# Attention with bias: k of seven pairs transposed by DMA, two more slots on VectorE, and a new order of work from slot 66 on

## The chip, the core and the metric

The kernel runs on one core of one Trainium2 chip. A core has five engines that run side by side: TensorE (PE in the profile, its weight loads PEld), VectorE (DVE), ScalarE (ACT), GpSimd (POOL) and SyncE (SP). Here SP only issues DMAs, and POOL issues those that convert from f32 to bf16 on the way. The metric is the device time of one execution in microseconds; the time given is the median of several runs.

## What is computed

Attention with an additive bias for 4 x 8 heads of 1024 rows and 64 columns, all in f32 at the interface:

```python
batch, n_heads, seq_len, head_dim = 4, 8, 1024, 64
scores = scale * np.matmul(q, k.transpose(0, 1, 3, 2))     # scale = 1/8
scores = scores + bias                                     # bias: [1, 1, 1024, 1024]
scores_max = np.max(scores, axis=-1, keepdims=True)
attn = np.exp(scores - scores_max) / (np.sum(np.exp(scores - scores_max), axis=-1, keepdims=True) + 1e-8)
return np.matmul(attn, v)
```

## The kernel before

Two heads form a pair; there are 16 pairs, in two groups of nine and seven (GROUPS). The queries of a head are cut into eight chunks of 128. One chunk of one head is a **slot**: 256 slots in all, numbered in the order in which the program lists them. The scores of a slot, 1024 keys by 128 queries, fill two PSUM banks. There are three such places (x = 0, 1, 2; tile pl, six banks). The slots of group 1, pairs 9 to 15, begin at 144: each pair has six there before the middle part of the group, so that pair 9 begins at slot 144, pair 10 at 150, and pair 15 at 180.

The whole program is one list of tokens, the string ORDER; each engine gets its instructions in the order of the list. The function do (line 607) turns a token into instructions. A number in a token is a slot, if nothing else is said:

- F and G fill the two banks of a slot with scores (fill, line 383; matmuls of line 376). A bank is not cleared between the slots that follow one another on a place: what the next slot needs is added to what is there, with operands made for that (keys of two neighbouring heads side by side with a negated query). For this, a pair has four arrays: ko and qo (k and q transposed), and ke and qe, which hold halves of ko and negated qo from neighbouring pairs. The slots that start afresh get the bias by line 373.
- X is one exponential on ACT over both banks (exp, line 399), written to E in bf16. P and Q split a round of three slots into two exponentials of three banks each.
- f, r, s, h, c, l are the six steps by which DVE computes an exponential instead of ACT (d_steps, line 409): f reads the scores from PSUM into dy, r takes the low half into de, s squares into ds, h shifts de in place, c multiplies ds by de, and l makes the bf16 result in de. Each step works on 128 x 1024 elements. In the kernel before, 29 slots are done in this way.
- A multiplies the exponentials of a slot with v (av, line 462) into a bank po that holds up to seven slots (SIZES); a column of ones in v gives the sums. "a" or "b" on the token opens the next bank, in one of two places in PSUM. R takes the reciprocals of a finished bank and M multiplies with them and issues the stores of the output, on SP (line 664). M's tile ob has four buffers.
- T and C make the transposed arrays: T transposes eight 128 x 128 blocks of the landed k or q on PE into PSUM (px, line 277), in one of the two places that the banks po also use; C copies px to ko on DVE, or to qo with a change of sign by halves. For pairs from 9 on (EARLY), C of k also issues the two copies of ko into ke as DMAs on SP (line 603). N negates q for pairs from 9 on and issues the copies to qe. D and S are DVE steps of the early pairs.
- L and U ask for the next load of the list LOADS; L ties the load to DVE's last instruction. The loads of q and k land in four buffers each (LANDS); a load of k of pair p is asked for only when pair p - 4 is marked as freed, which C does. The arrays ko, ke, qo and qe come from rings of nine buffers (RING).

What a T and a C do for one k of pairs 9 to 15 are thus eight transposes on PE, one copy of 128 x 1024 from PSUM on DVE, and the DMAs of ke on SP. In the order before, Tk9a and Ck9 stand between X98 and X102, and Tk15a and Ck15 around X161. On SP the DMAs are issued in the order of the list, and a DMA that waits holds up those behind it.

Of the kernel before, what the change touches and what calls it, by code (L numbers as in the profile page):

```python
# [8 lines left out]
F32 = mybir.dt.float32  # L9
# [11 lines left out]
A10a Sk4 X14 F16 Dk3p0 A9 G16 Dq3p0 Tk4b X15 Dq3p1 A6 Ck4 F17 G17 X16 A8 Sq4 F18 G18 Dk4p0 X17 Tq4b V2 F19 Cq4 G19  # L21
X18 A7 A12 Sk5 A11 F20 X19 R1 G20 Dq4p1 Tk5b M1 F21 X20 G21 Ck5 F22 A15a Sq5 X21 F23 Dq4p0 G22 G23 Tq5b V3 X22 A13
Cq5 A16 F24 X23 G24 Dk5p0 F25 G25 Dq5p0 A17 X24 F26 G26 Sk6 A14 f26 X25 F27 G27 Tk6b X27 F28 Dq5p1 G28 Sq6 A19 A18
X28 Ck6 F29 G29 F30 R2 Dk6p0 G30 X29 F31 M2 Tq6b V4 G31 X30 F32 Cq6 G32 A20a f32 X31 A21 F33 G33 Tk7b X33 Dq6p1 F34
G34 Dq6p0 A23 Ck7 X34 F35 G35 A28 r26 F36 X35 G36 Dk7p0 F37 G37 s26 Tq7b X36 A27 Cq7 A22 A29 X37 F38 V5 G38 F39 R3
Dq7p0 G39 X38 A25b h26 F40 M3 G40 A34 X39 c26 A24 F41 A30 Dq7p1 X40 A31 l26 G41 Tk8a X41 F42 F43 Ck8 G42 G43 X42 A26
f43 F44 G44 Tq8a X44 F45 Cq8 G45 F46 X45 G46 Dk8p0 F47 A35 Dq8p0 A33a V6 X46 G47 F48 R4 G48 M4 A41 X47 F49 Sr0 G49
f48 A40 A36 X49 F50 G50 Tr0b r43 X50 A38 F51 Cr0 G51 F52 X51 A39 Dr0p3 Dq6p2 F53 G53 r48 A37 X53 G52 F54 R5 r32 G54
X52 Sr1 F56 s43 G56 X54 Dr0p1 F55 s32 Tr1b X56 M5 G55 F57 h43 G57 X55 Cr1 F59 G59 A42a Dr1p0 A56 X57 Dr1p1 F58 h32
G58 f59 A46 X58 A44 F60 G60 A45 c32 X60 F61 G61 s48 A47 F62 X61 A54b R6 L U r59 G62 A49 F63 M6 L X62 F64 G64 l32 A50  # L30
X64 A55 G63 A53a h48 A62 X63 F65 R7 c43 G65 F67 G67 M7 X65 A61 c48 L U U A51 A52 F66 s59 X67 G66 F68 G68 A60 X66 f68
L F70 G70 A58 A63b X70 F69 l43 G69 F71 A57 X69 G71 F73 l48 A67 X71 F72 G72 A66 r68 G73 X72 F74 R8 h59 G74 X73 F75 f74
L G75 A65 X75 A48 F76 G76 M8 A64 X76 F77 R9 G77 s68 A73a F78 X77 G78 c59 L F79 G79 A69 l59 L U X79 A70 F80 G80 A76
X78 f80 F82 G82 A72 A75 X82 F81 M9 G81 F83 r74 G83 X81 F85 G85 f83 A43 A71b X85 F84 G84 A81 r83 X84 F86 G86 A78 Dq8p1
L U F88 X86 s74 G88 F87 G87 s83 A82 X87 A79 h74 L F89 G89 h68 L U A77 X88 A59 F90 R11 R10 c74 G90 X89 F91 M10 G91 X90
l74 F92 X91 G92 M11 A32a F93 r80 X92 G93 A87 A91 s80 F94 X93 G94 A85 h83 F95 c68 G95 X94 A92 A74 c83 A84 F96 X95 h80
G96 A89b R12 F97 M12 G97 X96 F98 c80 A90 G98 X97 A86 l68 A88 F99 G99 X98 Tq9a A94 Cq9 F100 X99 G100 A93 l80 A68 F101
X100 G101 F102 Tk9a R13 X101 M13 G102 F103 Nq9 L G103 A96b X102 Ck9 L F104 G104 A101 f104 A97 X103 F105 G105 Tk10a
X105 l83 F106 G106 F107 G107 X106 F108 f107 G108 A80 A100 X108 F109 G109 Ck10 A99 X109 F110 G110 r107 A95 F111 X110
R14 G111 M14 A98a F112 A106 r104 X111 G112 Tq10b A103 X112 Cq10 F113 G113 A109 F114 Nq10 X113 G114 s107 Tq11b F115  # L40
X114 Cq11 G115 F116 G116 h107 L A108 X115 F117 f116 L U G117 Tk12b X117 F118 G118 Ck12 A105 A102 X118 F120 R15 G120
s104 Tk11b X120 F121 M15 G121 F119 Ck11 L G119 X121 F123 G123 f119 A83a A112 X123 F124 G124 Tq12b c107 X124 F122 Cq12
G122 F126 A110 X122 l107 L U G126 A114 F127 X126 G127 A113 r119 F125 A111 X127 G125 s119 Tk13b F129 h104 X125 G129
Ck13 A115 F130 G130 R16 X129 Nq11 L A118b F128 Nq12 A124 c104 G128 X130 A117 A123 h119 L F132 r116 G132 X128 A121
A120 l104 X132 F131 G131 F133 M16 L G133 X131 F135 G135 A130 f135 L A126a X133 F134 G134 A122 X134 A127 R17 L s116
F138 G138 F136 M17 X138 G136 F137 G137 f136 Tk14b X137 F141 G141 A129 Ck14 X141 F139 G139 c119 F140 G140 Tq14b X139
h116 r135 A104 F144 X140 Cq14 L F142 G142 A125 r136 G144 X142 A128 A137b R18 L U U F143 s136 X144 G143 F145 c116 L U
G145 A107 X145 A133 s135 F147 A132 M18 G147 X143 A131 F148 l116 A138 G148 X147 F146 A134 G146 R19 Tq13a X148 M19 F150
G150 h135 A141b X146 h136 F151 G151 Cq13 L U U A139 A116 X150 c136 F149 G149 A140 l119 X151 F153 Tq15a X149 F154 Cq15
# [5 lines left out]
F178 l152 A171 X174 F173 G178 G173 R23 A168 X178 f173 F177 G177 A172 X177 F181 M23 G181 F176 G176 X181 F180 f176 G180
A152 A175 X180 F184 G184 r173 A174 X184 F179 G179 r176 F183 A181a r164 X179 A178 G183 F187 s173 X183 G187 R24 s176
F182 G182 X187 h173 A170 F186 s164 G186 X182 c173 F190 A179 M24 X186 F185 l173 G185 A180 A155 X185 G190 F189 h164
G189 A177 X190 h176 F188 c176 G188 X189 c164 A136b A135 R25 F193 l164 X188 G193 F192 A184 G192 X193 F191 l176 G191
A187 A185 X191 F196 G196 A183 f196 X192 F194 G194 A186 X194 F195 M25 G195 F199 R26 G199 X195 F197 f199 G197 A182a
A193 X197 F198 G198 F202 f198 G202 F200 X202 G200 r196 A173 X200 F201 G201 r199 F205 G205 X201 M26 A164 F203 A190  # L60
s199 A189 X205 F204 r198 G204 A192 s196 G203 X204 F208 G208 f203 A194b A188 X208 F207 G207 A197 R27 h196 X207 F206
G206 M27 F211 A201 h199 X206 A191 s198 G211 A202 F210 r203 X211 A200 G210 A205a c196 A204 X210 F213 l196 G213 F209
A176 X213 F212 G212 c199 A196 X212 A195 G209 l199 F215 X209 G215 F214 R28 R29 s203 X215 G214 h198 F216 X214 M28 G216
M29 F218 X216 A211b h203 F217 c198 G218 A210 X218 G217 l198 A207 F219 G219 X217 F221 G221 f219 A212 A208 X221 F220
G220 c203 F222 X220 G222 F224 r219 G224 A206 X222 f224 F223 G223 A213 A220a X223 F225 R30 r224 G225 A215 X225 F227
l203 F226 G226 A214 P226 F228 s224 A222 G228 G227 h224 A216 Q226 A221 M30 A209 F229 c224 G229 A218b R31 F230 X229
l224 G230 F231 G231 A228 X230 F232 f231 G232 A199 A217 X232 F233 G233 s219 F234 A223 X233 M31 G234 F235 r231 G235
X234 F236 G236 f235 A198 A203 X236 F237 G237 A225a r235 X237 F238 F239 h219 G238 A224 R32 s235 P238 G239 A227 F240
h235 G240 A233 c219 A226 Q238 F241 M32 G241 F242 A234 c235 A232 P241 A230b l235 F243 G243 G242 A239 A238 Q241 R33
A240 l219 F244 G244 A229 F245 M33 X244 G245 F246 s231 G246 A242 X245 f246 F247 G247 A243 A237a X247 F248 h231 G248  # L70
F249 r246 A236 X248 G249 R34 F250 M34 A235 X249 F251 s246 G250 A241 A244 P250 h246 F252 G251 c231 G252 A245 c246 A219
Q250 A247b l231 F253 G253 A249 A248 F254 X253 R35 G254 M35 F255 A250 G255 l246 X254 A231 A252 A251 X255 A254a R36
A246 M36 A253 A255 R37 M37
# [19 lines left out]
def kernel(  # L93
# [404 lines left out]
    with tc.manual_schedule():  # L498
# [108 lines left out]
        def do(token):  # L607
# [21 lines left out]
            elif kind == "C":  # L629
                pr, which, c0, n = pieces[name]  # L630
                copy_out(pr, which, c0, n, rests[name])
                if which:
                    for x in parts(pr, 1):
                        if pr >= EARLY or x == 1 and pr >= 2:
                            copy(pr, x, "ke", arrs[pr]["ko"])
                    freed.add(("k", pr))
                elif pr < NEGATED:
                    freed.add(("q", pr))
                more()
            elif kind == "D":  # L640
                piece, x = name.split("p")
                pr, which, c0, n = pieces[piece]
                double(pr, which, c0, n, int(x), vec)
            elif kind == "N":
                pr = int(name[1:])
                to = negate(pr)
# [6 lines left out]
            elif kind == "V":  # L653
                pr = int(name)
# [50 lines left out]
```

## Time and profile before

| What | us |
|---|---|
| median of 3 runs | 224.58 (224.04 to 224.98) |
| span of the profiled execution, first to last instruction | 222.3 |
| median of the runs less that span (launch and end, outside the span) | 2.3 |
| ACT busy | 211.5 |
| PE busy (ends of matmuls are modelled) | 214.3 |
| DVE busy | 204.6 |
| POOL busy | 71.5 |

The profile is a record of one execution. Busy time of an engine is the time in which at least one of its instructions runs, so instructions that overlap are not counted twice: the sum of a group's busy time can be less than its count by its mean. The views used are: the page (busy times, the chain of waits, groups of instructions by line and shape), the chain in order of time (start, duration, what), the timeline (start, duration, engine, line, operation, out<-in), the waits (who waited for whom: total us, times, longest), the DMA issues (count, KB each, median us from issue to landing), and windows (for a stretch, the busy time of PE, PEld, DVE, ACT and POOL with their counts, then the granted TensorE clock, the DMA share and GB/s). In a row of a group, what stands between the bars is its busy time in us and the mean ns of one; behind the second bar stands the idle time of the engine just before them, and what ended it. All DVE operations carry line 86, since one helper records them, and are told apart by their tiles.

### The profile page before, as it was taken

How to read it: one execution, taken by the hardware profiler on the slowest of the kernel's cores; microseconds unless marked ns; L12 is line 12 of the kernel's file. 1: busy time of each engine (PE TensorE's matmuls, PEld its weight loads, DVE VectorE, ACT ScalarE, POOL GpSimd, SP SyncE). 2: the span in 40 equal slices, each digit the busy share in tenths (PEclk: the TensorE clock that was granted, in tenths of full speed). 3: DMA queues.
4: the chain of work that ended last, by engine and by line, in shares of the span. 5: the costliest groups of instructions: out<-in, count | busy, mean ns of one | idle time of the engine just before them, and what ended most of it. 6: DMA issues, size and time to landing. Idle time of an engine off the chain costs nothing.

```text
span 222.3 us, 9048 instructions
## 1 busy us (share of the span) xinstructions
PE 214.3 (96%) x3965; PEld 197.3 (89%) x3965; DVE 204.6 (92%) x354; ACT 211.5 (95%) x229; POOL 71.5 (32%) x90
## 2 busy tenths in 40 slices
PE   7799999999999999999999999999999999999993
PEld 2689999989999999999998998898988999989992
DVE  2689989999999999999998999989998999999993
ACT  2799999999999999999999999999999999999992
POOL 8825346637346563030634445341000000000000
PEclk9999999999999999999999999999999999999998
DMA  5999999999999999669999999999111122011213
GB/s 170 229 205 218 224 237 170 159 169 185 138 150 128 127 114 156 79 87 208 126 191 199 192 101 144 182 188 99 44 43 32 38 62 66 8 44 47 82 43 109
DMA packets 86343, 28.87 MB, mean 130 GB/s; under 512 B 66400, under 2 KB 83040, under 8 KB 86304
## 3 DMA queue, kind: packets, MB, share of 16 engines
q0 software_dynamic: 62880, 14.06, 69.9%
q1 hardware_dynamic: 22720, 13.44, 22.3%
q10 hardware_dynamic: 704, 0.79, 1.2%
q8 instruction: 31, 0.51, 1.0%
q14 instruction: 8, 0.07, 0.1%
HBM read 29.36 MB, written 8.39 MB: 170 GB/s over the span
## 4 chain that ended last, share of the span: by engine, by line
ACT 79%; PE 11%; DVE 5%; DMA 2%; issue 0%; SPq 0%; DVEq 0%
ACT E L399 79%; PE pl L376 6%; PE po L462 2%; DMA dy<-in_k_dram 2%; DVE de L86 1%; PE pl L373 1%; DVE qe L86 1%; PE px L277 1%; DVE ds L86 1%; DVE dy L86 1%; DVE ko L86 0%; DVE ob L86 0%; PE px L283 0%; DVE qo L86 0%; DVE ke L86 0%
## 5 line engine op out<-in xcount | busy, mean ns | idle before, releaser
L399 ACT ACTIVATE E<-pl 128x1024 bf16<-128x1024 f32 (+2 forms) x225 | 208.6, 1109 | 1.9 <-PE pl L376 1.8
L462 PE MATMUL po<-vall,E 128*128 128x65 bf16 x1816 | 86.6, 194 | 0.1
L462 PEld LDWEIGHTS <-E 128*128 128x128 bf16 x1816 | 77.0, 98 | 2.5 <-ACT E L399 0.2
L376 PE MATMUL pl<-qo,ko 128*128 128x128 bf16 (+1 forms) x752 | 77.7, 239 | 1.0 <-ACT E L399 0.3
L376 PE MATMUL pl<-qe,ke 128*128 128x128 bf16 (+1 forms) x648 | 67.2, 239 | 0.5 <-DVE qe L86 0.2
L376 PEld LDWEIGHTS <-ko 128*128 128x128 bf16 x856 | 57.3, 98 | 7.0 <-ACT E L399 3.0
L376 PEld LDWEIGHTS <-ke 128*128 128x128 bf16 x648 | 43.5, 98 | 4.6 <-ACT E L399 1.9
L86 DVE TENSOR_SCALAR dy<-pl 128x1024 int32<-128x1024 f32 x29 | 35.4, 1220 | 4.0 <-PE pl L376 3.8
L86 DVE SCALAR_TENSOR_TENSOR de<-dy,ds 128x1024 uint16<-128x1024 int32 x29 | 35.0, 1217 | 0.2
L214 POOL DMA_DIRECT2D k<-in_k_dram x18 | 16.2, 901 | 25.2 <-DVE q L86 6.4
L251 POOL DMA_DIRECT2D vall<-in_v_dram x18 | 17.8, 993 | 19.4 <-DMA vall<-in_v_dram 5.2
L214 POOL DMA_DIRECT2D q<-in_q_dram x18 | 16.0, 891 | 22.3 <-DMA out_dram<-ob 8.5
L86 DVE TENSOR_TENSOR ob<-po,rs 128x448 f32<-128x448 f32 (+3 forms) x38 | 22.7, 601 | 0.4
L86 DVE TENSOR_SCALAR de<-dy 128x1024 f16<-128x1024 uint16 x29 | 20.1, 706 | 0.1
L86 DVE TENSOR_TENSOR ds<-de 128x1024 f16<-128x1024 f16 x29 | 19.5, 675 | 0.1
L86 DVE TENSOR_TENSOR ds<-ds,de 128x1024 f16<-128x1024 f16 x29 | 19.5, 680 | 0.0
L373 PE MATMUL pl<-ident,braw 128*128 128x128 bf16 x136 | 14.0, 227 | 0.0
L86 DVE TENSOR_SCALAR qo<-px,sgn 128x1024 bf16<-128x1024 bf16 (+2 forms) x18 | 12.3, 686 | 1.5 <-PE px L277 1.4
L86 DVE TENSOR_SCALAR de<-de 128x1024 f16<-128x1024 f16 x29 | 13.1, 459 | 0.2
L462 PE MATMUL po<-vall,de 128*128 128x65 bf16 x232 | 12.4, 194 | 0.5 <-DVE de L86 0.5
L373 PEld LDWEIGHTS <-braw 128*128 128x128 bf16 x136 | 11.8, 148 | 0.4
L86 DVE COPY ko<-px 128x1024 bf16<-128x1024 bf16 (+1 forms) x16 | 10.7, 668 | 1.4 <-PE px L283 1.1
(54 smaller groups left out, 125.9 us busy)
## 6 DMA issues: line engine op xcount, KB each, us to landing
ke<-ko SPq DMA_DIRECT2D x20, 128.0 KB, 4.3
k<-in_k_dram POOLq DMA_DIRECT2D x18, 128.0 KB, 5.7
q<-in_q_dram POOLq DMA_DIRECT2D x18, 128.0 KB, 4.4
out_dram<-ob SPq DMA_DIRECT2D x24, 96.0 KB, 2.9
vall<-in_v_dram POOLq DMA_DIRECT2D x18, 128.0 KB, 5.7
out_dram<-ob SPq DMA_DIRECT2D x32, 64.0 KB, 2.8
braw<-in_bias_dram POOLq DMA_DIRECT2D x7, 256.0 KB, 6.4
de<-in_v_dram POOLq DMA_DIRECT2D x7, 256.0 KB, 7.3
```

The costliest lines, as they stand in the source:

```text
L86: i = getattr(self.engine, name)(*args, **kwargs)
L214: return nc.gpsimd.dma_start(out=t[:, :, y, :], in_=(qf, kf)[x][pr][:, y].rearrange("p (c d) -> p c d", d=D))
L251: return nc.gpsimd.dma_start(out=vall[:, (2 * pr + t) % VR, :, :D], in_=vf[pr][:, t])
L277: m = nc.tensor.transpose(px[:, c, :], raws[pr, which, c0][:, c].rearrange("p t d -> p (t d)"), ident[:])
L373: m = nc.tensor.matmul(to, braw[:, c1, :].rearrange("p (kp kc) -> p kc kp", kc=NCH)[:, kc, :], ident8[:], start=i == 0 and order[0] == "b" ...
L376: m = nc.tensor.matmul(pl[:, 2 * x + b, i * P:(i + n) * P], kk[:, kc, :], qq[:, c:c + n, :].rearrange("p c q -> p (c q)"), start=i == 0 an ...
L399: read(nc.scalar.activation(E[:, e0:e0 + n].rearrange("p b x -> p (b x)"), pl[:, b0:b0 + n].rearrange("p b x -> p (b x)"), ACTF.Exp, scale ...
L462: nc.tensor.matmul(bank[b][:, banks[b].index(s), :], weights(s, kc), vall[:, slots[s][2] % VR, kc, :], start=first and kc == 0, stop=kc == ...
```

## The change

For pairs 9 to 15, T and C of k are gone from the list. A new token K issues one transposing DMA on SP, from the landed k straight into ko, and marks k as freed; a new token J issues the copies of ko into ke, as C did before.

```diff
+            elif kind == "K":
+                pr = int(name)
+                nc.sync.dma_start_transpose(out=arrays(pr)["ko"][:], in_=raws[pr, 1, 0].rearrange("p c t d -> p (c t d)"))
+                freed.add(("k", pr))
+                more()
+            elif kind == "J":
+                pr = int(name)
+                for x in parts(pr, 1):
+                    copy(pr, x, "ke", arrs[pr]["ko"])
```

In negate, the tile is taken from lands where it is there:

```diff
-        t = raws[pr, 0, 0].rearrange("p t c d -> p (t c d)").rearrange("p (c x) -> p c x", x=P)
+        t = (lands if (pr, 0, 0) in lands else raws)[pr, 0, 0]
+        t = t.rearrange("p t c d -> p (t c d)").rearrange("p (c x) -> p c x", x=P)
```

SIZES has 38 banks as before; three of them change by one or two slots. ORDER is the same up to A60 behind G68 and new from there on. The slots from 66 on that DVE computes are now 71, 77, 83, 92, 98, 104, 113, 119, 125, 134, 140, 146, 155, 161, 167, 176, 182, 188, 197, 203, 209, 219, 225, 231, 240 and 246, 26 in place of 24 (with 26, 32, 43, 48 and 59 before them, 31 in place of 29). There is no P and no Q any more: those rounds are single X. Some lines of the old list and of the new one:

```diff
-G96 A89b R12 F97 M12 G97 X96 F98 c80 A90 G98 X97 A86 l68 A88 F99 G99 X98 Tq9a A94 Cq9 F100 X99 G100 A93 l80 A68 F101
-X100 G101 F102 Tk9a R13 X101 M13 G102 F103 Nq9 L G103 A96b X102 Ck9 L F104 G104 A101 f104 A97 X103 F105 G105 Tk10a
...
-G162 X163 s155 A148 F161 R21 A153b M21 X162 F166 G166 l135 A156 A150 X166 G161 Tk15a h155 L F165 X161 Ck15 G165 F169
...
+G99 X97 F99 f98 A93 X99 A88b F100 G100 G101 A87 R12 F101 G102 F102 A86 c83 X100 G103 A99 K12 F103 X101 G104 F104 A43
+Dq8p1 X102 L L F105 G105 l92 X103 K11 r98 f104 A101 F106 U G106 M12 X105 G107 R13 s104 A96a F107 X106 A103 G108 s98 K9
+M13 X107 F108 h98 X108 A95 G109 l83 A77 A94 F109 Tq9b Cq9 F110 c98 s104 G110 X109 A100 A97 F111 G111 F112 X110 G112
+A107b R14 Nq9 X111 F113 A102 G113 J9 F114 G114 K10 M14 f113 L Tq10a X112 Cq10 F115 G115 r113 A111 J12 X114 F116 G116
+A110 G117 F117 X115 X116 F118 G118 Nq10 A105 A112 X117 L L F119 A92 J10 X118 s113 G119 G120 F120 X120 h104 h113 A106a
...
+X136 X137 A131 F138 F139 A136 c125 X138 l113 A124 G139 G140 F140 L c119 F141 Cq12 r134 G141 X139 f140 J11 U U A130b U
+A113 G142 F142 A139 X141 X142 F143 l119 G143 R18 F144 A128 A135 G144 l125 G145 F145 K13 X143 M18 A132 G146 X144 F146
+X145 A119 Nq12 f146 G147 F147 A133a A141 J14 F148 R19 r140 s134 G148 G149 X147 r146 X148 F149 A142 G150 X149 A145 s140
+M19 G151 F150 A138 A137 F151 A83 G152 R20 X150 h140 G153 F152 Tq13b h134 X151 M20 F154 G154 J13 X152 X154 Cq13 A148a
...
+l140 Nq13 G159 X160 A144 Cq14 c134 Nq14 F161 G161 A151 s146 G163 F163 K15 X159 f161 X163 Tq15b F162 Cq15 G162 X162
+r155 F164 G164 l134 Nq15 F166 A154b A149 G166 X164 F165 G165 A152 F167 R21 G167 A153 A160 X165 J15 f167 s155 M21 G168
+F168 A158 G170 F170 X166 G169 A165 F169 X168 h146 R22 X170 A162a A157 c146 F171 X169 G171 A156 G173 F173 h155 A164
```

K14, not among these lines, stands between G138 and X136. The q of pairs 9 to 15 is still transposed by T and C.

More of the change, by code (lines that the diff above doesn't have):

```diff
@@ L20 @@
 Sk3 F11 G11 Dq2p0 Tk3b Dq2p1 X10 A3 Sq3 F12 G12 X11 Ck3 A0 A4 A1 F13 X12 R0 G13 V1 Tq3b M0 F14 X13 G14 Cq3 F15 G15
[L21 to L24, printed above, removed]
@@ L30 @@
[L30 to L34, printed above, removed]
@@ L40 @@
[L40 to L49, printed above, removed]
@@ L55 @@
[L55 to L64, printed above, removed]
@@ L65 @@
[L65 to L73, printed above, removed]
+A10a Sk4 X14 F16 Dk3p0 A9 G16 Dq3p0 Tk4b X15 Dq3p1 A6 Ck4 F17 G17 X16 A8 Sq4 F18 G18 Dk4p0 X17 Tq4b V2 F19 Cq4 G19 X18
+A7 A12 Sk5 A11 F20 X19 R1 G20 Dq4p1 Tk5b M1 F21 X20 G21 Ck5 F22 A15a Sq5 X21 F23 Dq4p0 G22 G23 Tq5b V3 X22 A13 Cq5 A16
@@ new lines @@
+F50 G50 Tr0b r43 X50 A38 F51 Cr0 G51 F52 X51 A39 Dr0p3 Dq6p2 F53 G53 r48 A37 X53 G52 F54 R5 r32 G54 X52 Sr1 F56 s43
+G56 X54 Dr0p1 F55 s32 Tr1b X56 M5 G55 F57 h43 G57 X55 Cr1 F59 G59 A42a Dr1p0 A56 X57 Dr1p1 F58 h32 G58 f59 A46 X58 A44
+F60 G60 A45 c32 X60 F61 G61 s48 A47 F62 X61 A54b R6 L U r59 G62 A49 F63 M6 L X62 F64 G64 l32 A50 X64 A55 G63 A53a h48
+A62 X63 F65 R7 c43 G65 F67 G67 M7 X65 A61 c48 L U U A51 A52 F66 s59 X67 G66 F68 G68 A60 A58 A64b G70 U X66 G69 F69 X68
+X69 F70 U A63 X70 G71 F71 A65 A68 U G72 F72 U A57 G73 h59 X72 F73 c59 l48 f71 X73 L G74 F74 F75 G75 X74 A70 F76 R8 X75
@@ new lines @@
+M8 A48 G76 X76 F77 G77 L A69a l43 F78 G78 L A32 r71 R9 s71 A74 G79 f77 L X78 F79 F80 r77 G80 F81 G81 X79 A67 M9 X80
+A72 h71 A66 A78 G82 X81 F82 G83 l59 s77 F83 A76b F84 X82 G84 A79 A73 f83 F85 G85 R10 X84 G86 X85 F86 c71 G87 A75 h77
+M10 X86 r83 l71 A80 A85 F87 X87 A84 F88 G88 A81a X88 G89 F89 G90 U X89 F90 G91 c77 R11 F91 s83 L X90 G92 L L F92 X91
+G93 F93 h83 X93 A82 l77 f92 r92 s92 L G94 F94 F95 G95 F96 M11 h92 G96 A89 A91 X94 A71 G97 F97 X95 F98 A90 G98 X96 c92
+G99 X97 F99 f98 A93 X99 A88b F100 G100 G101 A87 R12 F101 G102 F102 A86 c83 X100 G103 A99 K12 F103 X101 G104 F104 A43
@@ new lines @@
+Dq8p1 X102 L L F105 G105 l92 X103 K11 r98 f104 A101 F106 U G106 M12 X105 G107 R13 r104 A96a F107 X106 A103 G108 s98 K9
+M13 X107 F108 h98 X108 A95 G109 l83 A77 A94 F109 Tq9b Cq9 F110 c98 s104 G110 X109 A100 A97 F111 G111 F112 X110 G112
+A107b R14 Nq9 X111 F113 A102 G113 J9 F114 G114 K10 M14 f113 L Tq10a X112 Cq10 F115 G115 r113 A111 J12 X114 F116 G116
+A110 G117 F117 X115 X116 F118 G118 Nq10 A105 A112 X117 L L F119 A92 J10 X118 s113 G119 G120 F120 X120 h104 h113 A106a
+c104 f119 A116 F121 R15 G121 A115 F122 X121 r119 l98 G122 F123 A109 G123 A120 X122 A108 G124 F124 X123 X124 s119 M15
@@ new lines @@
+F168 A158 G170 F170 X166 G169 A165 F169 X168 h146 R22 X170 A162a A157 c146 F171 X169 G171 A156 G173 F173 h155 A164
+G172 X171 A159 r167 M22 l146 F172 F174 X173 A170 G174 A163 X172 G176 F176 A134b G175 F175 A173 X174 r161 F177 G177
+f176 F179 A169 R23 X175 X177 M23 c155 s161 G178 F178 X178 G179 A166 l155 s167 A171 A146 G180 X179 F180 X180 r176 A172
+G181 A168a F181 G182 F182 X181 A174 G183 F183 A140 F184 G184 f182 F185 R24 h161 G185 X183 F186 G186 h167 X184 X185
+X186 c161 F187 G187 F188 G188 G189 F189 A175 s176 l161 M24 X187 f188 X189 G190 h176 F190 X190 A184 G191 F191 A181 c167
@@ new lines @@
+X235 R32 G236 F236 A232a G237 l225 A203 X236 F238 A233 G238 X237 G239 l231 A235 A227 X238 A228 F239 X239 F240 M32 G240
+G241 F241 f240 A237 A234b G242 F242 c219 R33 X241 A231 r240 G243 F243 M33 G244 A229 A238 F244 X242 G245 F245 X243 F246
+l219 X244 G246 A236 X245 f246 G247 F247 A209 A225 F248 G248 R34 X247 r246 s240 G249 F249 X248 A244a X249 A241 M34 F250
+h240 G250 G251 F251 A248 A219 G252 A249 X250 F252 s246 A247 X251 A245 F253 c240 G253 G254 X252 A243b A242 F254 A239
+A252 h246 l240 F255 X253 G255 R35 X254 c246 A250 M35 A251 A240 l246 X255 R36 A253a A254 A246 M36 A255 R37 M37
```

33 lines of the change are left out of this document (20 added, 13 removed).

## The prediction

> **What bounds the kernel now.** I read the page's shares first, then the chain of waits in order of time, then the sums of the stretch that the change rewrites.
>
> ```profile
> span 222.3 us, 9048 instructions
> ...
> PE 214.3 (96%) x3965; PEld 197.3 (89%) x3965; DVE 204.6 (92%) x354; ACT 211.5 (95%) x229; POOL 71.5 (32%) x90
> ...
> ACT 79%; PE 11%; DVE 5%; DMA 2%; issue 0%; SPq 0%; DVEq 0%
> ...
> 47.26 114.78 ACT E L399 x125
> ...
> 172.43 44.18 ACT E L399 x45
> ...
> 66.00:218.00 152.00, 151.00 (x2795) 140.00 (x2792) 146.51 (x231) 151.68 (x162) 35.26 (x39) 1.00 0.82 105
> ```
>
> The shares alone don't choose: three engines lie between 92% and 96%. The chain does. For 114.78 and again for 44.18 us it runs from one ACT exponential to the next and leaves ACT for nothing. The last row sums the stretch that the new order covers (slot 66 starts near 66 us, the last exponentials end near 218): PE, PEld, DVE, ACT and POOL in that sequence. ACT is busy 151.68 of 152.00 us and is the bound. DVE is busy 146.51 and idle 5.5. PE's 151.00 is flattered, since the ends of matmuls are modelled. The granted clock is 1.00 there, so no throttle enters. What follows the last exponential (one bank of four slots, one store) stays as it is.
>
> **The change: ACT.**
>
> ```profile
> L399 ACT ACTIVATE E<-pl 128x1024 bf16<-128x1024 f32 x213 | 196.4, 1103 | 1.0 <-PE pl L376 1.0
> ...
> L399 ACT ACTIVATE E<-pl 128x1536 bf16<-128x1536 f32 x8 | 11.2, 1516 | 0.0
> ```
>
> The mean of 1103 ns is not what one costs, as neighbours overlap: 196.4 / 213 = 0.922 us. The eight wide ones (P and Q in the order) cost 11.2 us for 12 slots, 0.933 each, so merging saved nothing. Before: 213 + 12 slots by ACT plus slots 0 and 1 in halves, 227. After: 223 single ones plus the same halves, 225. ACT's sum goes from 196.4 + 11.2 = 207.6 to 223 x 0.922 = 205.6: **-2.0 us**. No more than that can be gained while ACT feeds the chain.
>
> **VectorE.** The timeline of DVE (start, duration):
>
> ```profile
> 197.28 1.23 DVE L86 TENSOR_SCALAR dy<-pl 128x1024 int32<-128x1024 f32 x1
> 198.42 0.68 DVE L86 TENSOR_TENSOR ds<-de 128x1024 f16<-128x1024 f16 x1
> 199.02 0.62 DVE L86 TENSOR_TENSOR ob<-po,rs 128x448 f32<-128x448 f32 x1
> 199.55 0.68 DVE L86 TENSOR_SCALAR de<-dy 128x1024 f16<-128x1024 uint16 x1
> 200.15 1.22 DVE L86 TENSOR_SCALAR dy<-pl 128x1024 int32<-128x1024 f32 x1
> 201.40 0.69 DVE L86 TENSOR_SCALAR de<-dy 128x1024 f16<-128x1024 uint16 x1
> 202.01 0.42 DVE L86 TENSOR_SCALAR de<-de 128x1024 f16<-128x1024 f16 x1
> 202.34 0.20 DVE L86 RECIPROCAL rs<-po 128x7 f32<-128x7 f32 x1
> ...
> 204.08 0.62 DVE L86 TENSOR_TENSOR ob<-po,rs 128x448 f32<-128x448 f32 x1
> 204.61 0.68 DVE L86 TENSOR_TENSOR ds<-ds,de 128x1024 f16<-128x1024 f16 x1
> 205.33 1.23 DVE L86 SCALAR_TENSOR_TENSOR de<-dy,ds 128x1024 uint16<-128x1024 int32 x1
> 206.47 0.20 DVE L86 RECIPROCAL rs<-po 128x7 f32<-128x7 f32 x1
> ...
> L86 DVE COPY ko<-px 128x1024 bf16<-128x1024 bf16 x15 | 10.3, 685 | 1.4 <-PE px L283 1.1 <-PE px L277 0.3
> ```
>
> An operation starts before its predecessor's recorded end, so I count from start to start. The six steps of a slot (f r s h c l) take 198.42 - 197.28 = 1.14, 200.15 - 199.55 = 0.60, 199.02 - 198.42 = 0.60, 202.34 - 202.01 = 0.33, the second tensor_tensor, of the same shape as the first, 0.60, and 206.47 - 205.33 = 1.14: 4.41 us. Two slots more: **+8.82**.
>
> The copies of k out of PSUM (Ck9 to Ck15) go: seven times 0.685, less the overlap of 0.68 - 0.60 = 0.08, so 0.60 each: **-4.20**.
>
> The overlap is lost where an operation needs the result of the one right before it. From f to r of one slot, 200.15 to 201.40 takes 1.25 in place of 1.14; from c to l, 204.61 to 205.33 takes 0.72 in place of 0.60. I take 0.11 each. In DVE's own sequence from slot 66 on, the old order has 25 such neighbours (c59 l59, f83 r83, r80 s80, R12 M12, R13 M13, R14 M14, Cq10 Nq10, r119 s119, R19 M19, R21 M21, s152 h152, R22 M22, h176 c176, c196 l196, c199 l199, c198 l198, s224 h224, f235 r235, s235 h235, c235 l235, R34 M34, s246 h246, R35 M35, R36 M36, R37 M37). The new one has 12 (s59 h59, h59 c59, R8 M8, f77 r77, s83 h83, f92 r92, r92 s92, h92 c92, R23 M23, R31 M31, R36 M36, R37 M37). 13 fewer: **-1.43**.
>
> DVE together: 8.82 - 4.20 - 1.43 = +3.2, that is 146.5 + 3.2 = 149.7 us. With ACT's two microseconds gone the stretch would be 150.0 long. So both would be full, and what DVE still waits decides. If w is that idle time, the stretch ends after 149.7 + w, and never under 150.0.
>
> ```profile
> DVE dy L86 <- PE pl L376: 3.4, 9, 0.6
> DVE qo L86 <- PE px L277: 0.5, 2, 0.4
> DVE rs L86 <- PE po L462: 0.3, 1, 0.3
> ```
>
> These are DVE's waits between 66 and 218 us: nine times it stood before a scores tile that PE had not finished. DVE was then the engine with time to spare; PE could not fill a bank that ACT still read. When DVE itself is late, PE has the scores ready before it arrives, so I expect most of the 3.4 to go, bounded by zero and by 5.5 (all of today's idle). I take **w = 0.9**: a stretch of 150.6, **-1.4 us**.
>
> **PE and the transposes.**
>
> ```profile
> 29.39 0.45 PE px L277 x8
> ...
> ke<-ko SPq DMA_DIRECT2D x20, 128.0 KB, 4.3
> ...
> k<-in_k_dram POOLq DMA_DIRECT2D x6, 256.0 KB, 7.5
> ...
> q0 software_dynamic: 62880, 14.06, 69.9%
> ...
> SPq L664 <- DVE ob L86: 73.2, 26, 6.9
> ```
>
> Eight transposes take 0.45 us of PE in the chain; seven pairs less make -3.15 us, more than ACT loses, so PE gets no tighter. They go to seven DMAs of 256 KB inside SBUF (K), and no row shows such a DMA. The nearest is ke<-ko: SBUF to SBUF, half the bytes, 4.3 us. A 256 KB load needs 7.5. The low end is therefore 4.3. For the far end: if each 2-byte element were a packet, at the 0.699 x 16 x 222.3 / 62880 = 0.0395 us of one engine that a packet of q0 takes, 131072 / 16 x 0.0395 = 324 us. I take 8, near the ke row, since whole rows are read here as well.
>
> That would be hidden. A slot lasts 152 / 190 = 0.80 us. K15 stands near slot 160 and its first scores (F180) near slot 180: 16.0 us. J15, the copies of ke behind it, takes 4.3 of these, so K15 has 11.7. K13 and F168 lie 24 slots apart, K14 and F174 36, K12 and F163 59, K11 and F157 51, K10 and F150 38, K9 and F144 36. K15 is the first to be late. On SP's queue each J waits for its K, and output stores stand behind it (M21 behind J15). SP has idle time for that, as 73.2 us of it go in waits for finished outputs alone; four output buffers, each filled once in seven slots, cover some 22 us. K also waits on SP until the raw k has landed and, in a ring of nine, PE has done with an old ko buffer: K9 takes that of pair 2, last read by slot 107, where K9 stands. The loads behind a raw buffer (k13 behind K9) wait for the transposing read now; k13 is asked for at slot 107 and K13 comes at 143, 28.8 us later. The ke copies, the q transposes and the number of loads stay. The edit in negate changes nothing for pairs from 9 on. I cost all of this at nothing, under the cover just named.
>
> The Trainium skill speaks against the swap: "VectorE: DVE Perf Modes", in "The three transpose paths" and its rules for authors, gives 390 ns for a 128x128 transpose on TensorE and 1309 ns by the DMA crossbar, and keeps the DMA for cases where a PSUM destination won't do. This trace has 0.45 us for eight on TensorE, below the page's figure. By the page an estimate for K is 8 x 1.309 = 10.5 us, and the sum would stay as it is, with 1.2 us left of K15's 11.7.
>
> **The rivals.** (1) *DVE becomes the bound and keeps a good part of its waits.* Slower from w = 2.3 on (149.7 + 2.3 = 152.0). With all 5.5 kept, 155.2: +3.2 us, 227.8. For it: DVE would be filled to 99%, and an f, an R or an M needs PE in order. Against: its waits now are those of an engine with time to spare. (2) *An even exchange*: w between 1.2 and 3.4, the stretch within 1.1 us of today's, 223.5 to 225.7. (3) *K is late.* Decides from 11.7 us; with 20 us, F180 waits 8 us, and PE, then ACT, stand still: 223.2 + 8 = 231, far more with packets per element. For it: no row shows the operation, and the loads fill the DMA queues until 160 us. Against: the copies of ke land in 4.3 beside the same loads. That K takes nothing off DVE and PE can be ruled out, as the instructions are gone.
>
> **How the numbers follow.** The profiled span of 222.3 lies 2.3 us under the median of the runs, 224.58; I take these as a constant. Forecast: 224.58 - 1.4 = **223.2**, with ACT's limit at 224.58 - 2.0 = 222.6. A measurement of this kernel can tell 0.5%, 1.1 us. Chances: forecast (w up to 1.2, faster by over 0.5%) 0.46; even exchange 0.33; DVE's waits beyond that 0.14; K late 0.07. So faster 0.46, within 0.5% 0.33, slower 0.21. The range reaches from 221.9 (ACT's limit less the runs' own scatter of 0.5 to 0.9) to 227.8 (all of DVE's waits kept); K late lies outside it.
>
> **What would show it.** ACT: 223 wide-1024 exponentials, some 205.6 us busy. DVE: busy up by about 3, its idle time from slot 66 on under 2 us, and the chain crossing to DVE more often than its 5% now. PE waits for ko or ke on SP's DMA: none. K: landing under 11.7 us. The prediction is wrong if the chain shows a landing K or ke, if waits of dy for pl remain at 3 us, or if ACT has idle gaps that add up to more than 1 us between slots 66 and 255 with DVE idle at the same time.

## The result, and the profile after

| | before | after |
|---|---|---|
| median of the runs shown with the result, us | 224.78 (224.04 to 225.32) | 232.38 (231.82 to 233.87) |
| span of the profiled execution, us | 222.3 | 230.0 |

The kernel after is **slower**: 1.0366 times the time before, 95% interval 1.0332 to 1.0400, or 7.6 us. The forecast was 223.2, its range 221.9 to 227.8. Some executions of a kernel are clearly slower than its others; the ratios leave them out and the medians don't, so sizes are read from the ratios where the two differ. The page of the kernel after, with its busy times, granted clock by slices, and shares of the chain of waits:

```profile
PE 214.7 (93%) x3909; PEld 196.2 (85%) x3909; DVE 207.9 (90%) x359; ACT 211.0 (92%) x231; POOL 70.5 (31%) x90
...
PEclk9999999999999999999999999958999999999998
...
PE 49%; ACT 35%; DMA 7%; DVE 6%; SPq 2%; issue 1%; DVEq 0%
```

and its DMA issues (count, KB each, median us to landing; the transposing form has no size):

```profile
out_dram<-ob SPq DMA_DIRECT2D x47, 64.0 KB, 3.1
out_dram<-ob SPq DMA_DIRECT2D x93, 32.0 KB, 2.9
ke<-ko SPq DMA_DIRECT2D x20, 128.0 KB, 5.3
...
ko<-k SPq DMA_TRANSPOSE x7, 5.3
```

The engines do what was forecast: DVE is busy 207.9 - 204.6 = 3.3 us longer, ACT 0.5 us less, PE has 56 instructions fewer. But the chain no longer stays on ACT (35%, 79% before); DMA and SP's queue (SPq) are in it. The first of the two slices in which the granted clock falls begins at 149.5 us. K lands after 5.3 us, and the copies of ke now need 5.3 where they needed 4.3. To see where the time went I cut both traces where equally many slots have begun. The orders differ, so slots are counted here as their exponentials start, from 0: number 66 starts at 65.6 (before) and 65.8 us (after), number 155 at 137.1 and 136.1 (between two of ACT's, at 135.6 and 136.5), and number 185 at 160.9 and 168.4. The last cut is made a little ahead of number 185, at 157 and 165 us; ACT does 23 exponentials in both middle windows. First the windows of before, then those of after (PE, PEld, DVE, ACT, POOL, then granted clock, DMA share, GB/s):

```profile
66.00:137.00 71.00, 70.56 (x1298) 65.89 (x1296) 68.87 (x109) 71.00 (x78) 28.27 (x31) 1.00 1.25 143
137.00:157.00 20.00, 19.81 (x361) 18.01 (x360) 18.49 (x29) 20.00 (x23) 6.99 (x8) 1.00 1.31 146
157.00:218.00 61.00, 60.63 (x1143) 56.10 (x1140) 59.15 (x96) 60.68 (x63) 0.00 (x0) 1.00 0.17 48
```

```profile
66.00:136.00 70.00, 69.16 (x1245) 63.15 (x1243) 69.17 (x109) 69.94 (x78) 25.04 (x29) 1.00 1.31 146
136.00:165.00 29.00, 21.52 (x368) 19.71 (x367) 19.90 (x31) 20.80 (x23) 10.12 (x11) 0.88 1.49 162
165.00:226.00 61.00, 60.74 (x1133) 56.18 (x1131) 60.52 (x98) 60.58 (x66) 0.00 (x0) 1.00 0.20 48
```

Up to number 155 the kernel after is a microsecond *faster*. The last stretch takes the same 61 us. All of the loss lies in the middle: 29 us for the work of 20, with ACT busy 20.80 of them. There PE waited for data, 7.4 us in all; the waits of after (before has no such wait there):

```profile
PE pl L376 <- DMA qe<-q: 4.7, 1, 4.7
...
PE po L462 <- DMA vall<-in_v_dram: 2.7, 1, 2.7
```

The second is v of pair 10, the first qe of pair 13. What held qe is in the timeline of SP's queue (start, duration, what, how many):

```profile
136.48 8.17 SPq L673 DMA_DIRECT2D out_dram<-ob  x12
144.69 1.11 SPq L603 DMA_DIRECT2D ke<-ko  x2
145.97 3.52 SPq L603 DMA_DIRECT2D qe<-q  x4
```

and in the chain in order of time:

```profile
138.49 5.33 DMA out_dram<-ob
...
143.84 0.33 SPq L673
...
144.69 0.47 SPq L603
...
145.97 6.57 DMA qe<-q
...
152.66 1.01 PE pl L376 x4
```

N13 was done on DVE at 138.5 us. Its copies to qe stood behind twelve stores of banks 19 and 20. So qe was issued at 145.97, 7.5 us late, landed 6.57 later, and PE started at 152.66. In the kernel before, nine stores had gone out ahead of the copies of N13, and SP stood idle when these came:

```profile
129.54 4.32 SPq L664 DMA_DIRECT2D out_dram<-ob  x9
...
135.90 5.29 SPq L603 DMA_DIRECT2D qe<-q  x5
```

Most of the 8.17 us is the issuing itself: these nine stores, almost without a wait, took 4.32 us, 0.48 each, so an estimate for twelve is 5.8. The other 2.4 are waits. SP's DMAs go round over eight semaphores in the trace, and one whose semaphore is still in use waits until that earlier DMA has landed: the chain has a store that took 5.33 us.

Three things had changed around this place. *Stores*: a bank's outputs are joined into a store where slots are neighbours in the output, and the new order mixes the slots more; counted from ORDER and SIZES, 160 stores in place of 117. *Lead*: from N13 to the first F of pair 13 there were 13 slots before (152 to 165) and 8 after (159 to 167); Cq9 and Nq9 moved from slots 99 and 102 to 109 and 111, so that q9's landing buffer, and with it the load of q13 and all loads behind it, came free later; and v of pair 10 is first used at slot 158, not 161. The trace has the load of q13 issued at 108.3 us (105.6 before) and that of v10 at 134.2 (130.2), landed 141.0 (134.4). *The transposing form*, which the experiments weigh.

### The profile page after: what moved, and what is told of

The parts are those of the page before. It is cut to its first block, busy times and chain, and to the rows that moved or that the text cites. A ratio compares the mean times of both kernels' runs of the same rounds, so it can differ in the third digit from the quotient of the medians.

```text
span 230.0 us, 9009 instructions
## 1 busy us (share of the span) xinstructions
PE 214.7 (93%) x3909; PEld 196.2 (85%) x3909; DVE 207.9 (90%) x359; ACT 211.0 (92%) x231; POOL 70.5 (31%) x90
## 3 DMA queue, kind: packets, MB, share of 16 engines
q1 hardware_dynamic: 36048, 15.28, 30.1%
## 4 chain that ended last, share of the span: by engine, by line
PE 49%; ACT 35%; DMA 7%; DVE 6%; SPq 2%; issue 1%; DVEq 0%
ACT E L399 35%; PE pl L376 28%; PE po L462 16%; DMA qe<-q 3%; PE pl L373 2%; DMA out_dram<-ob 2%; DMA dy<-in_k_dram 2%; PE px L276 2%; DVE de L85 1%; DVE dy L85 1%; SPq L673 1%; DVE qe L85 1%; DVE ds L85 1%; SPq L603 0%; DVE ko L85 0%
## 5 line engine op out<-in xcount | busy, mean ns | idle before, releaser
L399 ACT ACTIVATE E<-pl 128x1024 bf16<-128x1024 f32 (+1 forms) x227 | 208.0, 1084 | 10.6 <-PE pl L376 8.2
L462 PE MATMUL po<-vall,E 128*128 128x65 bf16 x1800 | 84.8, 195 | 2.8 <-DMA vall<-in_v_dram 2.7
L376 PE MATMUL pl<-qe,ke 128*128 128x128 bf16 (+1 forms) x648 | 69.2, 242 | 5.4 <-DMA qe<-q 4.7
L85 DVE TENSOR_SCALAR dy<-pl 128x1024 int32<-128x1024 f32 x31 | 37.7, 1218 | 3.8 <-PE pl L376 3.3
L85 DVE SCALAR_TENSOR_TENSOR de<-dy,ds 128x1024 uint16<-128x1024 int32 x31 | 37.5, 1213 | 0.1
L250 POOL DMA_DIRECT2D vall<-in_v_dram x18 | 16.5, 916 | 22.6 <-DMA vall<-in_v_dram 13.5
L85 DVE TENSOR_TENSOR ob<-po,rs 128x448 f32<-128x448 f32 (+2 forms) x38 | 22.8, 600 | 0.3
L85 DVE TENSOR_SCALAR de<-dy 128x1024 f16<-128x1024 uint16 x31 | 22.2, 716 | 0.1
L85 DVE TENSOR_TENSOR ds<-de 128x1024 f16<-128x1024 f16 x31 | 20.9, 678 | 0.1
L85 DVE RECIPROCAL rs<-po 128x7 f32<-128x7 f32 (+2 forms) x38 | 7.5, 196 | 6.9 <-PE po L462 6.6
```

What stands on the lines that cost most here:

```text
L85: i = getattr(self.engine, name)(*args, **kwargs)
L250: return nc.gpsimd.dma_start(out=vall[:, (2 * pr + t) % VR, :, :D], in_=vf[pr][:, t])
L376: m = nc.tensor.matmul(pl[:, 2 * x + b, i * P:(i + n) * P], kk[:, kc, :], qq[:, c:c + n, :].rearrange("p c q -> p (c q)"), start=i == 0 an ...
L399: read(nc.scalar.activation(E[:, e0:e0 + n].rearrange("p b x -> p (b x)"), pl[:, b0:b0 + n].rearrange("p b x -> p (b x)"), ACTF.Exp, scale ...
L462: nc.tensor.matmul(bank[b][:, banks[b].index(s), :], weights(s, kc), vall[:, slots[s][2] % VR, kc, :], start=first and kc == 0, stop=kc == ...
```

## The experiments

Ratios are against the kernel before, timed beside each run.

### The first four: one suspect at a time

**e1_held**: the twelve stores wait until the qe copies of pair 15 are issued.

```diff
-                    w.dma_start(out=to, in_=of_)
+                    if b in (19, 20): held.append((to, of_))
+                    else: w.dma_start(out=to, in_=of_)
...
+    if pr == 15: for to, of_ in held: nc.sync.dma_start(out=to, in_=of_)
```

> Theory A (SP's queue): the new banks hold slots that join into fewer, longer stores no more, 160 stores in place of 117, and the twelve of banks 19 and 20 stand on SP ahead of the copies of q of pair 13, which then land 4.7 us late. Here those twelve stores are issued behind the copies of q of pair 15; all else is as in the changed kernel. A expects PE's wait for qe of pair 13 (4.7 us) and the cold clock behind it to be gone, the wait for v of pair 10 (2.7 us) to stay: 225 to 227. Theory B (the transposing DMA itself delays what shares the DMA queues with it): the wait stays, 231 to 233. Theory C (VectorE's load is the bound): the same, 231 to 233.

230.84 us, ratio 1.0295 (1.0261 to 1.0328): theory A's time, 225 to 227, is missed. The wait for qe is gone, and the same place now waits for v:

```profile
PE po L462 <- DMA vall<-in_v_dram: 5.9, 2, 3.6
```

**e2_held_v10**: also `"v9", "v10", "k15", "q15"` in LOADS, where v10 stood behind q15.

> As e1_held, and v of pair 10 is loaded ahead of k and q of pair 15. Theory A: both waits are gone, and what is left is the gain that ACT showed up to slot 155, 1.0 to 1.4 us: 222.8 to 224.2. B: 229 to 233. C: 228 or more, with DVE busy without a gap from slot 155 on.

230.85, 1.0270 (1.0209 to 1.0331). v waits 1.5 us, but PE now stands 2.4 us before the transposes of a q that lands late. The wait went one load further, and A's time, up to 224.2, is missed again.

**e3_fewer_stores**: `stores[:3] if b >= 9 else stores`.

> The changed kernel, but each bank from 9 on issues at most three of its stores (109 in all instead of 160), so part of the output isn't stored. Theory A: SP's queue runs as freely as before the change, the copies of q are issued within 1 us of their data, the loads behind q's buffers come earlier too, both waits are gone: 222.5 to 224.5. B: the waits stay, 230 to 233. C: 228 or more.

230.07, 1.0247 (1.0202 to 1.0292): 1.2% of the 3.7% go with the stores, where A had all of it (up to 224.5). PE still waits 3.7 us for v.

**e4_k_only**: the order, banks and 29 slots of before; T and C of k of pairs 9 to 15 are replaced by K and J.

```diff
-Tk9a ... Ck9 ... (to Tk15a Ck15)
+K9 ... J9 ... (to K15 J15)
```

> The order, the banks and the 29 slots of before, with K and J in place of T and C for k of pairs 9 to 15: 117 stores. Theory A: the transposing DMAs are hidden where SP has room, ACT stays the bound: 224 to 225.5, the same as before. B: slower than before by 3 us or more, 228 or more. C: VectorE loses 4.2 us of copies and nothing else, so 224 to 225.

226.32, 1.0091 (1.0059 to 1.0123). So K alone makes the old order slower too, by 0.9% or some 2.0 us, although DVE has 4.20 us of copies less. That is more than theory A had (up to 225.5) and less than B (228 or more).

### What the transposing form does to its neighbours

**f1_deeper**: e2 with five loads under way in place of three from the load where k13 begins.

> As e2_held_v10, with five loads under way from k of pair 13 on instead of three. Theory D (a chain of loads, each issued when the third before it has landed; the longer landings of about 6.5 us in place of 5.3 add up along it, until v and q of pairs 10 to 13 are late): the chain shortens, v of pair 10 is on time, 224 to 227. Theory E (the 16 DMA engines themselves are full in this stretch): loads only land later each, 229 to 232, as e2_held_v10.

233.52, 1.0425 (1.0394 to 1.0455), worse than both ranges: the loads of v then landed after 8.0 us in the median and 12.6 at most, where the kernel after has 5.9 and 7.9. More of them under way don't come sooner.

**f2_dummy_transposes** and **f3_dummy_copies**: the kernel before, whole, and behind Ck9 to Ck15 one more DMA of the same 256 KB that nothing reads.

```diff
+spare = side.tile([P, NCH, 2, D], BF, name="side").rearrange("p c t d -> p (c t d)")
+nc.sync.dma_start_transpose(out=spare.rearrange("p (c x) -> p c x", x=P), in_=raws[pr, 1, 0]...)   # f2
+nc.sync.dma_start(out=spare, in_=raws[pr, 1, 0]...)                                                # f3
```

> The kernel before with everything it does, and seven transposing DMAs more, one at each Ck9 to Ck15, from the landed k into a spare tile that nobody reads. Theory B (a transposing DMA slows the loads beside it): what e4_k_only lost comes back without any other change: 225.5 to 227.5, with loads from k15 to v13 landing after 6 to 7 us instead of 5.3. If the loss of e4_k_only came from waits in its own order (J behind K on SP): 224 to 225.

> As f2_dummy_transposes, with plain DMAs of the same 256 KB in place of the transposing ones. If the transposing form with its packets of 256 bytes is what costs: 224 to 225. If any 256 KB more in SBUF costs as much: 225.5 to 227.5.

f2 231.52, 1.0317 (1.0277 to 1.0357); f3 224.84, 1.0040 (1.0005 to 1.0075). f3 came out as expected, f2 far above its 225.5 to 227.5. The bytes, the number of issues and the buffer are the same; the form costs 2.8%, some 6.2 us. The landing times of these DMAs differ by a microsecond, as the rows of DMA issues show, first of f2, then of f3:

```profile
side<-k SPq DMA_TRANSPOSE x7, 5.4
```

```profile
side<-k SPq DMA_DIRECT2D x7, 256.0 KB, 4.4
```

What differs is what happens to the rest. Three windows of f2 around 114 us (last columns: DMA share and GB/s of the whole core):

```profile
113.00:114.25 1.25, 1.25 (x25) 1.21 (x23) 1.22 (x4) 1.25 (x3) 0.00 (x0) 1.00 3.26 116
114.25:115.50 1.25, 1.25 (x28) 1.17 (x26) 1.25 (x5) 1.25 (x2) 0.00 (x0) 1.00 0.23 8
115.50:116.75 1.25, 1.25 (x34) 1.23 (x31) 1.25 (x4) 1.25 (x3) 0.13 (x1) 1.00 2.13 160
```

For 1.25 us the core moves 8 GB/s between 116 and 160, though copies of ke and loads of k were under way. At 114.8 us, 22 packets of 256 bytes were in flight, eight of which took over 2.1 us; between 95 and 155 us, 61 packets of this size took over 0.3 us, and none did in f3. The kernel after has 67 such packets, g1 below, with plain copies, none. (By the packets of the two runs, a transposing DMA of 256 KB is cut into 1024 packets of 256 bytes, the plain one into 128 of 2048.) In the chain of f2 transfers beside it land late, one behind the other: a copy of ke after 6.51 us (4.3 in the median of before), then one of qe, then a load of q, for which PE waits:

```profile
113.33 6.51 DMA ke<-ko
...
125.62 6.44 DMA qe<-q
...
133.55 4.86 DMA q<-in_q_dram
```

The row of that wait:

```profile
PE px L277 <- DMA q<-in_q_dram: 4.7, 1, 4.7
```

The Trainium skill ("Advanced Engine Details and Errata", "X-Bar Transpose (TRN2)") says that these DMAs are as fast as regular ones. For the DMA's own landing the trace has 5.4 against 4.4 us, somewhat slower; for the whole kernel f2 against f3 does not agree. One more thing differs between these two: SP takes 1.51 us in the median to issue a transposing DMA and 0.51 for a plain one. Its share of the cost is not told apart.

**f4_more_stores**: the kernel before with its stores from bank 9 on cut smaller, 157 in place of 117, the same bytes.

> The kernel before with its stores from bank 9 on cut into pieces of at most two chunks of one head, 157 stores in place of 117, the same bytes. Theory A (the number of stores on SP costs about what e3_fewer_stores gave back, 2.3 us): 225.5 to 227.5. If stores are hidden as long as the order leaves SP room ahead of the copies: 224 to 225.

226.48, 1.0108 (1.0089 to 1.0128): forty more stores cost that order 2.4 us, though SP still waits 62.8 us for finished outputs there.

### The same in the new order

**g1_plain_copy**: the form alone goes, everything else in the kernel after stays.

```diff
-nc.sync.dma_start_transpose(out=arrays(pr)["ko"][:], in_=raws[pr, 1, 0]...)
+nc.sync.dma_start(out=arrays(pr)["ko"][:].rearrange("p c x -> p (c x)"), in_=raws[pr, 1, 0]...)
```

> The kernel after, whole, except that the seven DMAs K write their 256 KB as a plain copy instead of transposing them (so k of pairs 9 to 15 is left unturned and the scores of these pairs aren't the reference's; every issue, wait, copy, matmul and store stays). Theory T (the transposing form is the main cause): the two dummy runs differ by 228.2 - 222.5 = 5.7 us in span and about 6.7 in the median; without it the kernel after goes from 232.4 to about 225.7 (224.5 to 227.5), the waits of PE for qe and for v fall from 7.4 us to under 3, and no DMA packet of 256 bytes takes over 1 us. Rival S (the new order, its 43 more stores and its fuller queue of SP are the cause, a transposing DMA is one more 256 KB copy): 231 to 232.4, and the waits for qe and v stay.

230.15, 1.0241 (1.0173 to 1.0309). A miss for my theory: 1.25% of the 3.7% goes, some 2.8 us, where I had 6.7.

**g2_plain_few**: g1 with e3's edit.

> The kernel after with plain copies as K (as in the run before) and with at most three output stores for each bank from bank 9 on (the rest of the output of these banks is not stored). Theory T with the stores as second cause: both are gone, so the sum of the forecast is left, 2.0 us of ScalarE and at most 1.4 of waits below the kernel before: 221 to 223.3. Rival (the order itself loses elsewhere, whatever the DMAs do): 225 or more, the same as the run with plain copies alone within 1 us.

229.00, 1.0209 (1.0162 to 1.0255). A miss as well. 2.1%, some 4.7 us, stays with both gone, and PE still waits for v of pair 10 (3.7 us in its waits).

**g3_old_order_plain**: e4 with plain copies.

> The order of before with k of pairs 9 to 15 taken through K and J (226.3 with transposing DMAs, +2.1 us against before), here with plain copies in their place (k of these pairs is left unturned). Theory T: K's form costs this order several us and the 7 ko copies of VectorE that are gone (7 x 0.60 us) give some back: 220 to 224.5, faster than or equal to before. Rival (an order that wasn't made for K loses by its late ke, not by the transfers): 226 or more.

223.98, 1.0001 (0.9976 to 1.0025), against 1.0091 for e4: in the old order the form costs 0.9%. The 4.20 us that DVE saves gain nothing there; ACT stays the bound.

### The order's own lead

**h1_q9_k9_early** and **h2_early_plain** (h1 with plain copies): the list between slots 97 and 107.

```diff
-X99 A88b ... K11 F106 ... K9 M13 ... Tq9b Cq9 ... Nq9
+X99 Tq9b Cq9 Nq9 K9 A88b ... F106 ... K11 M13 ...
```

> The kernel after with four pieces of its order moved: the transposes, copy and negation of q of pair 9 and K of pair 9 stand ahead of A88 (slot 97; they stood at slots 109 to 111 and 107, q9 of the kernel before at 99 to 102), and K of pair 11 takes the place that K of pair 9 had. So the landing tiles of k9 and q9 come free some 10 us earlier, and the loads of k13 and q13, which the ones up to v15 stand behind, can go out earlier. Theory O (the new order itself frees the landing tiles late and uses v and q of the pairs early, so that its chain of loads is late whatever form K has): q13 goes out before 105.6 us (108.3 now), v10 before 131 (134.2 now), and 2 to 5 us of the stall between slots 155 and 180 go: 227.5 to 230.5. Rival (transfers beside the loads alone): the chain is limited by the landing times from slot 112 on, so v10 goes out at 133 or later, and the time stays at 231.5 to 232.5.

> The order of the run before this one (q9 and K9 early) with plain copies as K (k of pairs 9 to 15 left unturned). Theory O: with the chain of loads earlier and its transfers unblocked, most of the stall goes, 224 to 227, and PE's waits for q and v are under 2 us. Rival (the stall is a matter of the place of the A and F steps, not of the loads): 229 or more, as with plain copies alone (230.2).

232.49, 1.0361 (1.0334 to 1.0387), and 232.60, 1.0377 (1.0361 to 1.0392): the times stayed, so theory O is missed. The waits of h1 say why. PE waits 0.2 us for v now; the stores in front of qe, which the wait for v had covered in part, cost their full time:

```profile
PE pl L382 <- DMA qe<-q: 7.0, 1, 7.0
...
PE po L468 <- DMA vall<-in_v_dram: 0.2, 1, 0.2
```

**k1_early_held**, **k2_early_held_plain**: h1 and h2 with e1's edit. **k3_held_past_ke**, **k4_held_past_ke_plain**: the held stores go out behind J15, not behind N15.

> The kernel after with two edits that each did nothing or little alone: q9 and K9 early (232.5 alone; v of pair 10 then came in time, PE still waited 7.0 us for qe of pair 13), and the 12 output stores of banks 19 and 20 held on SP until the qe copies of pair 15 are issued (230.8 alone; qe then came in time, PE waited 5.9 us for v). Theory C (two waits stand behind each other at one place, slots 158 to 169: the loads of v, and the 12 stores in front of the qe copies on SP; whichever goes, the other takes its time): with both edits neither is left: the stall between slots 155 and 180 shrinks to before's 19 to 22 us (28.7 now), 223.5 to 227. Rival (the transposing DMAs' blocked packets hold whatever comes next, so that a third wait takes the place): 229 or more.

> As the run before, with plain copies as K (k of pairs 9 to 15 left unturned). Theory C with the transposing form costing about 2 us where nothing else is late: 222 to 225 and 1 to 3 us under the run with transposing DMAs. Rival (the form matters only through the loads, which now have slack): the same as the run before within 1 us.

> q9 and K9 early as before, and the 12 output stores of banks 19 and 20 held until the ke copies of pair 15 are issued too (held until the qe copies of pair 15 alone, they took SP from 145.7 to 153.7 us and pair 15's ke copy came 2.6 us late). Theory C (SP's queue of stores in front of copies that PE waits for): no wait of PE for qe or ke is left; with the transposing DMAs v stays late by some 3 us: 225.5 to 228.5. Rival (blocked transfers take the next place): 229 or more.

> The same with plain copies as K (k of pairs 9 to 15 left unturned). Theory C: v is in time as in the run with plain copies before (v10 landed at 132.7 and 134.7 us), nothing else is late, and the forecast's own sum comes out: 221.9 to 223.8, under the kernel before. Rival (a further cause in the order): 225 or more.

k1 230.59, 1.0325 (1.0258 to 1.0393); k2 227.69, 1.0141 (1.0088 to 1.0193); k3 231.20, 1.0317 (1.0266 to 1.0368); k4 229.89, 1.0271 (1.0239 to 1.0303). With the form, v is late again (PE waits 3.2 us in k1, 7.2 in k3). Without it, v is in time and the held burst hits what stands behind it. SP in k2:

```profile
145.69 8.05 SPq L669 DMA_DIRECT2D out_dram<-ob  x12
153.78 0.49 SPq L609 DMA_DIRECT2D ke<-ko  x1
```

PE stood 2.6 us at that place, until 158.1. The profile names a store as what ended the wait; I read it as this ke, 4.3 us after its issue, which is not shown. In k4, DVE waits 2.3 us for an output buffer that a held store still reads. Moving the stores moves the stall. All four missed what I expected, k4 by 6 us.

**h3_all_three**: q9 and K9 early, plain copies, and at most three stores per bank; so the stores are taken out, not moved.

> The new order with all three suspects out at once: q9 and K9 early, plain copies as K (k of pairs 9 to 15 left unturned) and at most three output stores per bank from bank 9 on (the rest of the output of these banks is not stored); no store is held. Theory C (late loads, the transposing form and the stores in front of SP's copies are all of it): the forecast's own sum is left, 221.5 to 224, no more than the kernel before, and at slot 185 the progress is at or before 160.9 us. Rival (something else in the order between slots 155 and 185 loses, such as the nearness of F and A to their data): 226 or more.

224.66 us, **1.0017 (0.9993 to 1.0041)**. That is 0.7 us above theory C's range and well below the rival's 226. Slot number 185 starts at 160.0 us, as theory C had it. The stall is gone, as its windows show:

```profile
65.00:137.00 72.00, 70.40 (x1261) 63.85 (x1258) 69.78 (x111) 70.72 (x78) 29.02 (x32) 1.00 1.26 146
137.00:157.00 20.00, 19.85 (x372) 18.41 (x370) 19.88 (x32) 20.00 (x23) 6.53 (x8) 1.00 1.38 165
157.00:217.50 60.50, 60.25 (x1125) 55.73 (x1122) 59.95 (x97) 60.17 (x66) 0.00 (x0) 1.00 0.12 29
```

So with the three suspects out together the whole loss against the kernel before is gone, and they don't add up. From 1.0366, the early q9 takes nothing alone, the form 1.25%, the stores 1.2%, form and stores 1.6%, early q9 and form nothing, all three 3.5%. In the combinations tried, something else is late next as long as one of them is left.

Two things stay open. h3 stores fewer bytes as well as fewer times (12.99 in place of 15.28 MB on SP's and ACT's queue), so the number of stores is told apart by f4 alone, in the old order. And early q9 with few stores but with transposing DMAs was not tried: what the form costs in this order when nothing else is late isn't known; in six pairs of kernels that differ in the form alone (after/g1, h1/h2, k1/k2, k3/k4, e4/g3, f2/f3) it was between nothing and 2.8%. No version was faster than before.

## Why the prediction was wrong, step by step

- **ACT, -2.0 us: right.** The 223 exponentials are busy 206.0 us; forecast 205.6.
- **DVE, +3.2: right.** +3.3 on the page. (In the lines of the new list shown above, the step behind R13 is r104.) Outside the stall DVE's idle time is 70.00 - 69.17 and 61.00 - 60.52, 1.3 us, where it was 2.13 + 1.85 in the same two stretches; the forecast was under 2. Rival 1 (DVE keeps its waits) did not happen.
- **The sum, -1.4: supported, not shown.** After gains 1.2 us from number 66 to 155. From number 66 to 255 h3 takes 151.2 us, before 151.4; but in h3 ACT waits 1.28 us in one piece near slot 100, where q9 was put early, a wait that after does not have. Less that, h3 would take 149.9, 1.5 us under before (an estimate from these figures). No run shows it whole: h3's end, behind number 255, takes 6.5 us, that of before 5.3, and why stays open.
- **PE, -3.15: right and without effect**, as costed.
- **K's landing, 8 us (4.3 to 324): too high, on the harmless side.** 5.3, each under 7; the estimate from the Trainium skill's figure, 10.5, was further off. Rival 3 named K as the one to be late from 11.7 us on. PE never waited for ko or ke; SP did, in front of two J, 5.3 us in all. That this rival's 231 lies near the measured 232.4 is chance.
- **The step that failed** is "The ke copies, the q transposes and the number of loads stay", and with it "I cost all of this at nothing, under the cover just named." The *numbers* of copies and loads stayed; their places did not. I worked out the lead of seven K's against their first F, but not that of N against F (8 slots for pair 13, some 6.4 us at 0.80 each, where qe alone took 6.57 to land), nor where the landing buffers come free, nor v's first use. I never counted the stores, which a new composition of the banks changes from 117 to 160. And "SP has idle time for that, as 73.2 us of it go in waits for finished outputs alone" took an average over the kernel for the 14 us, from N13's end at 138.5 to PE's start at 152.7, in which SP was needed. Twelve stores took 8.17 us of it there. With the stores, the early q9 and the form changed together (h3), the time was that of before; with any one of the three changed alone, at least 2.4% of the 3.7% stayed.
- **What K does to other transfers was a missing term.** The far end of its bounds (324 us) priced the DMA by itself; that the transfers beside it nearly stop was neither bounded nor a rival. It would have been a rival on the slower side: e4 against g3 gives its price in the old order, 0.9% or some 2.0 us.
- Of the signs named in advance, gaps of ACT over 1 us while DVE idles came true (in the middle window ACT is idle 8.2 us and DVE 9.1). A landing came into the chain, but that of qe and of a store, not of K or ke. DVE's waits of dy for pl stayed at 3.3 us, 2.5 of them in one piece.

## What to carry to other kernels

When a list of work is ordered anew, count for every transfer the time from its issue to its first use, with what stands ahead of it in its queue, and count the transfers themselves again: what is hidden is hidden by a lead, not by a queue's idle time over the whole kernel. A wait that is removed shows the next one behind it, so several small causes at one place must be taken out together before any of them is called harmless. A transfer moved to a DMA is to be priced by what it does to the transfers beside it too; a dummy of the same bytes in the old kernel gives a first size of that, though here it cost 2.8% and the form in the new order 1.25%.

## What the runs showed of the hardware

A transposing DMA of 256 KB inside SBUF landed after 5.4 us where a plain one took 4.4, but the whole core's DMAs nearly stopped for 1.25 us beside one. Twelve stores of 32 or 64 KB kept SP for 8.17 us: some 0.48 us each for the issue, the rest waits for earlier DMAs to land, as eight semaphores go round.

After a wait of PE the granted clock fell, which made the stall longer than the wait. Four matmuls of one shape ahead of the stall and behind it, from the timeline of PE in the kernel after, and a window:

```profile
143.24 0.60 PE L376 MATMUL pl<-qe,ke 128*128 128x256 bf16 x4
...
152.66 1.01 PE L376 MATMUL pl<-qe,ke 128*128 128x256 bf16 x4 [4.74 <-DMA qe<-q]
```

```profile
145.00:155.00 10.00, 5.26 (x81) 4.67 (x79) 4.95 (x9) 4.59 (x5) 3.41 (x5) 0.73 1.44 171
```

The granted clock is 0.73 over these 10 us, 0.50 from 152.6 to 155.0, and 1.00 from 140.0 to 147.9. The Trainium skill ("TensorE: Matmul & The Clock Gate", "What's actually happening") has the clock at half speed after an idle window of about 3.4 us; the wait of 4.74 us is longer than that, and the trace agrees. In k2 a wait of 2.62 us, shorter than that window, was enough: the granted clock was 0.54 from 158.1 to 160.0 behind it. There the measurement decides.
